# Gate products, last blocks and last mix of a two-layer encoder: three PSUM and queue edits

## The chip, the core and the metric

One NeuronCore of a Trainium2 chip runs the whole program in one launch. The metric is the device time of that launch in microseconds (us), lower is better. The core has five engines, each with its own in-order queue, that meet through semaphores: TensorE (PE in the profile, with its weight loads as PEld), VectorE (DVE), ScalarE (ACT), GpSimd (POOL) and SyncE (SP), which here only issues DMAs. Matmuls write to PSUM, which VectorE and ScalarE can read.

## The reference

One inference step of a two-layer encoder over 640 tokens (512 of a prompt, 8 x 16 of samples), model width 1024, all in float32:

```python
for l in range(2):
    h = rmsnorm(x, ln1);  u, va, qkv, z, b, a, ga, gb = split(h @ w_in)
    z_a = gelu(u) * spatial(layernorm(gelu(va)))        # branch A: chunked gMLP
    z_b = rmsnorm(gated_delta_rule(conv(qkv), ...)) * silu(z)   # branch B
    mix = sigmoid(ga) * (z_a @ p_a) + sigmoid(gb) * (z_b @ p_b)
    x = x + mix @ w_o
    x = x + square(relu(rmsnorm(x, ln2) @ w_up)) @ w_down
y = rmsnorm(x, final_norm)
```

This case is about the line `mix`, the product with `w_o` and the end of the product with `w_down`.

## The kernel before

Activations lie transposed: 1024 features as 8 chunks of 128 partitions, 640 tokens along the free axis, in two halves of 320 (`HT`). Every large product takes each operand as a high and a low part (`split`: ScalarE writes the high part, then VectorE writes the rest as the low part), and sums three matmuls: high x high, high weight x low activation, low weight x high activation. A block is 128 output features for all tokens: 2 halves x 8 chunks x 3 = 48 matmuls of 320 columns (`three`, called by `gemm`). A block's weights (512 KB) are loaded by SP into `raw` (three buffers) and split into `whi` and `wlo` (two buffers each), one block ahead of their use (`Feed`). So ScalarE can write a block's `whi` only when TensorE has finished the block two ahead of it.

PSUM has 8 banks: the tag `g` is a pair of two-bank tiles (`pair`, names `pg_...`), and the tags `c` and `d` are two one-bank tiles each (`bank`, names `ps_...`). A `gemm` fills a pair, one half of the tokens in each bank; two pairs take turns, so a block may start when the block two ahead of it has been read out of PSUM. All waits are kept per tile.

TensorE's order is the order of the program. The other engines' orders come from a scheduler with priorities: what stands in `tc.high_priority(offset=...)` is taken earlier by so many steps, the splits of weights among it.

The places of this change, in the order of the program, each once in a layer:

- `merge`, first loop (stage pb): `z_b @ p_b` in eight blocks. A gate tile `sg` (name `rg`) is loaded from the DRAM tensor `gd` by `gated`, and VectorE multiplies block `g` in PSUM by it into `mix[g]` (L1036). The gates of blocks 0 and 1 are loaded through GpSimd's queue. Ahead of this loop on VectorE runs the layer norm of branch A (L977 to L981, tile `vn`), whose powers GpSimd computes (L979).
- `merge`, second loop (stage pa): `z_a @ p_a`; VectorE multiplies by the other gate (L1046), GpSimd adds the product to `mix[m]` (L1047), and `split` writes chunk `m` of `Bh` and `Bl`.
- `residual_raw` (stage wo): `mix @ w_o`, whose every block needs all eight chunks of `Bh` and `Bl`. `take` adds a block to `x`, scales it (`hwo`), splits it into `Ah` and `Al` and adds its squares into the sum of the norm, the first seven blocks as a whole and the last one in two halves of 320 tokens. `rates` follows, within the first block of the stage up.
- `residual` (end of stage dn): the last 1024 rows of `w_down`, blocks 0 to 3 by `gemm`, and 4 to 7 by `group`: token half `a` = 0 first, then `a` = 1, each as two pair tiles (`i` = 0 and 1) that hold two blocks (`j` = 0 and 1) of that half. `add` adds a pair to `x`, squares it on ScalarE and sums the squares into `acca`, on GpSimd for half 0 and on VectorE for half 1. `finish` then computes the rate of a half (three small products `ps_msa`, a power on GpSimd, a spread `dga`, three products `ps_mra`) and scales that half: for layer 0 into the `Ah` and `Al` of the next layer's first stage (gf), for layer 1 into the output.

Of the kernel before, what the change touches and what calls it, by code (L numbers as in the profile page):

```python
# [11 lines left out]
AF = mybir.ActivationFunctionType  # L12
ALU = mybir.AluOpType
# [8 lines left out]
KC = 8  # L22
# [8 lines left out]
HT = NT // 2  # L31
# [8 lines left out]
AHEAD = 200  # L40
# [22 lines left out]
def encoder(ctx, tc, xin, wblk, wba, sct, sdelta, prow, pcol, gates, wst, bsr, convw, consts, delta0,  # L63
            y_out, conv_out, dp_out, ds_out, gv_out):
    nc = tc.nc
# [12 lines left out]
    def mm(out, lhsT, rhs, start, stop, pos=None):  # L78
        kw = {} if pos is None else {"tile_position": pos}
        nc.tensor.matmul(out, lhsT=lhsT, rhs=rhs, start=start, stop=stop, **kw)  # L80


    x = cp.tile([P, KC, NT], F32, name="x")
# [9 lines left out]
    half = (slice(0, HT), slice(HT, NT))  # L93
# [38 lines left out]
    def split(dst_hi, dst_lo, src):  # L132
        nc.scalar.activation(dst_hi, src, AF.Copy)  # L133
        nc.vector.tensor_tensor(dst_lo, src, dst_hi.bitcast(F32), op=ALU.subtract)  # L134
# [44 lines left out]
    def bank(tag, nm):  # L179
        return psp.tile([P, 512], F32, tag=tag, name=f"ps_{nm}")  # L180

    def pair(nm):
        return psp.tile([P, 2, 512], F32, tag="g", bufs=2, name=f"pg_{nm}")

    def three(ps, w, ah, al):

        hi, lo = (v[:].rearrange("p (k c) -> p k c", k=KC) for v in w)
        for a in range(2):
            n = slice(a * 320, (a + 1) * 320)
            for k in range(KC):  # L190
                mm(ps[:, a, :320], hi[:, k, :], ah[:, k, n], k == 0, False)
                mm(ps[:, a, :320], hi[:, k, :], al[:, k, n], False, False)
                mm(ps[:, a, :320], lo[:, k, :], ah[:, k, n], False, k == KC - 1)
                yield

    def gemm(l, b, ah, al, nm, use, halves=False):

        w = feed.take(l, b)
        ps = pair(nm)
        for u, _ in enumerate(three(ps, w, ah, al)):  # L200
            if halves and u % 8 == 7:
                use(ps, u // 8)
            elif u == 15:
                use(ps)
            yield

    def group(l, bs, ah, al, nm, use, pl, chunks=False):


        w = [feed.take(l, bs[0]), feed.take(l, bs[1], ahead=False)] + [feed.apart(l, b, pl) for b in bs[2:]]  # L210
        w = [[v[:].rearrange("p (k c) -> p k c", k=KC) for v in p] for p in w]
        order = [(j, k) for k in range(KC) for j in range(2)] if chunks else [(j, k) for j in range(2) for k in range(KC)]
        for a in range(2):
            for i in range(2):
                ps = pair(f"{nm}{a}{i}")
                for u, (j, k) in enumerate(order):
                    hi, lo = w[2 * i + j]
                    mm(ps[:, j, :HT], hi[:, k, :], ah[:, k, half[a]], k == 0, False)
                    mm(ps[:, j, :HT], hi[:, k, :], al[:, k, half[a]], False, False)
                    mm(ps[:, j, :HT], lo[:, k, :], ah[:, k, half[a]], False, k == KC - 1)  # L220
                    if (a, i, u) == (1, 1, 1):
                        feed.ahead()
                    if u % 2 and u < 15:
                        yield
                use(i, a, ps)
                yield

    def paced(work, n, ahead=AHEAD):
# [388 lines left out]
    halves = (slice(0, 64), slice(64, 128))  # L617
# [171 lines left out]
    v2 = lambda ap: ap.rearrange("p (a n) -> p a n", a=2)  # L789
# [160 lines left out]
    def merge(l, ond, msd, gd):  # L950
        with phase(f"merge{l}", 1) as pl:
            Bh = pl.tile([P, KC, NT], F32R, name=f"Bh{l}")
            Bl = pl.tile([P, KC, NT], F32R, name=f"Bl{l}")
            with phase(f"branch{l}", 1) as po:
# [9 lines left out]
                bs = rep_row(po, bsr[l], f"bs{l}", "bs")  # L964
# [42 lines left out]
                    run(zs)  # L1007

                with phase(f"sp{l}", 1) as pq:
                    def gated(i, m, eng=nc.sync):  # L1010
                        sg = pq.tile([P, NT], F32, tag="sg", bufs=3, name=f"rg{i}{l}{m}")
                        eng.dma_start(sg[:], gd[i, m])
                        return sg

                    def spatial(g):
                        u = gated(0, g)
                        b0, b1 = bank("dc"[g % 2], f"s{l}{g}a"), bank("dc"[g % 2], f"s{l}{g}b")
                        for t in range(5):
                            o = b0[:, t * P:(t + 1) * P] if t < 4 else b1[:, 0:P]
                            mm(o, vn[:, t, g * P:(g + 1) * P], ws[:, t // 4, g, :], True, True)  # L1020
                        s = pq.tile([P, NT], F32, tag="s", bufs=2, name=f"sp{l}{g}")
                        nc.vector.tensor_tensor(s[:, 0:512].rearrange("p (t n) -> p t n", t=4),
                                                b0[:].rearrange("p (t n) -> p t n", t=4), rep(bsv[:, g, :], 1, 4), op=ALU.add)
                        nc.vector.tensor_tensor(s[:, 512:640].rearrange("p (b n) -> p b n", b=8),
                                                b1[:, 0:P].rearrange("p (b n) -> p b n", b=8), rep(bsv[:, g, 0:16], 1, 8), op=ALU.add)
                        nc.gpsimd.tensor_tensor(s[:], s[:], u[:], op=ALU.mult)
                        split(Ah[:, g, :], Al[:, g, :], s[:])

                    with tc.high_priority(offset=2 * AHEAD):
                        ahead = [gated(1, g, nc.gpsimd) for g in range(2)]  # L1030
                    mix = [pq.tile([P, NT], F32, name=f"mix{l}{g}") for g in range(KC)]
                    for g in range(KC):
                        sg = ahead[g] if g < 2 else gated(1, g)

                        def pb(ps):
                            nc.vector.tensor_tensor(v2(mix[g][:]), ps[:, :, 0:HT], v2(sg[:]), op=ALU.mult)  # L1036

                        run(gemm(l, WB_PB + g, Bh, Bl, f"pb{l}{g}", pb))
                        for i in {3: (0, 1), 4: (2, 3), 5: (4, 5), 6: (6, 7)}.get(g, ()):
                            spatial(i)  # L1040
                    nc.sync.dma_start(gv_out[l], vn[:, 4, :])
                    for m in range(KC):
                        sg = gated(2, m)

                        def pa(ps):
                            nc.vector.tensor_tensor(v2(sg[:]), ps[:, :, 0:HT], v2(sg[:]), op=ALU.mult)  # L1046
                            nc.gpsimd.tensor_tensor(mix[m][:], mix[m][:], sg[:], op=ALU.add)  # L1047
                            split(Bh[:, m, :], Bl[:, m, :], mix[m][:])

                        run(gemm(l, WB_PA + m, Ah, Al, f"pa{l}{m}", pa))  # L1050
            es = ExitStack()
# [3 lines left out]
    def residual(l, b0, ah, al, nm, nrm):  # L1055

        def add(xs, ps, dst, first):
            nc.vector.tensor_tensor(xs, ps[:, :, 0:HT], xs, op=ALU.add)
            nrm.add(dst, xs, first, nc.vector if dst == 1 else nc.gpsimd)

        for m in range(4):
            run(gemm(l, b0 + m, ah, al, f"{nm}{m}", lambda ps: add(v2(x[:, m, :]), ps, None, m == 0)))
        with phase(f"g{nm}") as pw:
            g = group(l, range(b0 + 4, b0 + 8), ah, al, nm,
                      lambda i, a, ps: add(x[:, 4 + 2 * i:6 + 2 * i, half[a]], ps, a, False), pw)
            for _ in range(16):
                next(g)
            run(g, fin := nrm.finish(0))
            run(fin)
        return nrm.finish(1)  # L1070

    def residual_raw(l, b0, ah, al, nm, nrm):

        def take(m, n, ps, w, dst, eng):
            xs, h = w(x[:, m, n]), nrm.pl.tile([P, NT], F32, tag="h", bufs=2, name=f"h{nm}{m}")[:, n]
            nc.vector.tensor_tensor(xs, ps, xs, op=ALU.add)
            nrm.scaled(h, m, n)
            split(Ah[:, m, n], Al[:, m, n], h)
            nrm.add(dst, xs, m == 0, eng)

        for m in range(KC - 1):
            run(gemm(l, b0 + m, ah, al, f"{nm}{m}",
                     lambda ps: take(m, slice(0, NT), ps[:, :, 0:HT], v2, None, nc.gpsimd)))
        m = KC - 1
        run(gemm(l, b0 + m, ah, al, f"{nm}{m}",
                 lambda ps, a: take(m, half[a], ps[:, a, 0:HT], lambda v: v, a, nc.vector), halves=True))

        def rates():
            for n, a in ((1, 0), (2, 1)):
                for _ in range(n):  # L1090
                    yield
                yield from nrm.rate(a, 5)

        return rates()
# [148 lines left out]
```

## Time and profile before

| | us |
|---|---|
| Median of 3 runs (2514.13 to 2517.27) | 2514.52 |
| The profiled execution | 2513.98 |
| Span of its trace, first to last instruction | 2512.3 |
| TensorE busy, 98% of the span, 18456 matmuls | 2464.4 |
| VectorE, ScalarE and GpSimd busy | 1300.4, 1026.6 and 568.3 |
| Start of the stages pb, pa, wo and up in layer 0 | 612.39, 684.52, 740.84 and 800.47 |
| Start of the stages pb, pa, wo and up in layer 1 | 1852.58, 1924.19, 1980.51 and 2040.13 |
| Start of the stage gf of layer 1 | 1257.56 |

Busy time on TensorE is time in which a matmul is in flight; a matmul lasts about 0.31 us from its start to its end, and the next one starts 0.147 us after it where nothing waits. The idle time in brackets of a row is what the engine stood idle ahead of it, and after the arrow stands what ended that. `PEclk` is the TensorE clock that was granted, as a share of full speed. The start of a row is in us from the start of the span.

### The profile page before, as it was taken

Reading aid. Unit: us, or ns where it says so; the run is one execution under the profiler, and the core shown is the slowest. Engines: PE = TensorE matmul, PEld = TensorE weight load, DVE = VectorE, ACT = ScalarE, POOL = GpSimd, SP = SyncE. Lnnn points to the kernel's source line nnn. Section 1 sums busy time; section 2 is a strip of 40 time slices with the busy share of each in tenths; the row PEclk is TensorE's granted clock in tenths of the full one; section 3 lists DMA queues with packets and bytes.
Section 4 is the critical chain, followed back from the end, with each engine's and each line's share of the span. In section 5 each row is a group of like instructions: output and inputs, shape, how many; then the busy total and the mean of one; then the engine's idle time right before and its main releaser. Section 6 shows DMA issues by size and latency. Waiting matters only on the chain. (4 is left out here: it accounts for less than half of the span.)

```text
span 2512.3 us, 45051 instructions
## 1 busy us (share of the span) xinstructions
PE 2464.4 (98%) x18456; PEld 2387.2 (95%) x18456; DVE 1300.4 (52%) x2686; ACT 1026.6 (41%) x1968; POOL 568.3 (23%) x638
## 2 busy tenths in 40 slices
PE   8999999999999999999999999999999999999998
PEld 7999999998999999999999999999989999999997
DVE  6656776527455433333346677664275553333333
ACT  5767666533123212122347676774322222122122
POOL 0233433211222201011213343331112221011012
PEclk9999999999999999999999999999999999999999
DMA  5233333346532222222233333343564322222221
GB/s 175 83 107 122 103 96 99 115 132 228 167 95 74 72 75 74 76 76 76 85 94 115 102 96 96 101 127 113 164 204 145 92 68 76 76 76 76 73 71 67
DMA packets 124493, 261.28 MB, mean 104 GB/s; under 512 B 17232, under 2 KB 57072, under 8 KB 124288
## 3 DMA queue, kind: packets, MB, share of 16 engines
q1 hardware_dynamic: 123968, 257.10, 32.3%
q8 instruction: 145, 2.38, 0.4%
q0 software_dynamic: 320, 1.31, 0.2%
q14 instruction: 60, 0.49, 0.1%
HBM read 218.22 MB, written 40.15 MB: 103 GB/s over the span
## 5 line engine op out<-in xcount | busy, mean ns | idle before, releaser
L133 ACT ACTIVATE whi<-raw 128x1024 fp32r<-128x1024 f32 x304 | 321.8, 1059 | 1003.9 <-issue 369.6
L134 DVE TENSOR_TENSOR wlo<-raw,whi 128x1024 fp32r<-128x1024 f32 x304 | 397.8, 1309 | 167.8 <-ACT whi L133 153.6
L80 PE MATMUL pg_dn<-gl,whi 128*128 128x320 f32 x1024 | 316.6, 309 | 2.1 <-DVE gl L1111 2.1
L80 PE MATMUL pg_up<-Ah,whi 128*128 128x320 f32 x1024 | 317.1, 310 | 0.0
L80 PE MATMUL pg_dn<-gh,whi 128*128 128x320 f32 x1024 | 316.8, 309 | 0.0
L80 PE MATMUL pg_up<-Ah,wlo 128*128 128x320 f32 x1024 | 316.4, 309 | 0.0
L80 PE MATMUL pg_dn<-gh,wlo 128*128 128x320 f32 x1024 | 316.4, 309 | 0.0
L80 PE MATMUL pg_up<-Al,whi 128*128 128x320 f32 x1024 | 316.4, 309 | 0.0
L80 PE MATMUL pg_g<-Ah,whi 128*128 128x320 f32 x896 | 289.4, 323 | 1.3 <-ACT sg L821 1.3
L80 PE MATMUL pg_g<-Ah,wlo 128*128 128x320 f32 x896 | 276.9, 309 | 0.1
L80 PE MATMUL pg_g<-Al,whi 128*128 128x320 f32 x896 | 276.4, 308 | 0.0
L1110 POOL TENSOR_TENSOR r<-r 128x640 f32<-128x640 f32 x64 | 101.8, 1590 | 684.8 <-ACT gh L1109 684.8
L80 PE MATMUL pg_p<-Ah,whi 128*128 128x320 f32 x768 | 251.4, 327 | 0.0
L80 PE MATMUL pg_p<-Al,whi 128*128 128x320 f32 x768 | 237.0, 309 | 0.4 <-DVE Al L134 0.4
L80 PE MATMUL pg_p<-Ah,wlo 128*128 128x320 f32 x768 | 237.3, 309 | 0.0
L80 PEld LDWEIGHTS pg_dn<-gl,whi 128*128 128x128 f32 x1024 | 192.2, 188 | 2.6 <-DVE gl L1111 2.6
L80 PEld LDWEIGHTS pg_up<-Ah,whi 128*128 128x128 f32 x1024 | 192.2, 188 | 0.0
L80 PEld LDWEIGHTS pg_up<-Al,whi 128*128 128x128 f32 x1024 | 192.2, 188 | 0.0
L80 PEld LDWEIGHTS pg_dn<-gh,whi 128*128 128x128 f32 x1024 | 192.2, 188 | 0.0
L80 PEld LDWEIGHTS pg_dn<-gh,wlo 128*128 128x128 f32 x1024 | 192.2, 188 | 0.0
L80 PEld LDWEIGHTS pg_up<-Ah,wlo 128*128 128x128 f32 x1024 | 192.2, 188 | 0.0
L80 PEld LDWEIGHTS pg_g<-Ah,whi 128*128 128x128 f32 x896 | 168.6, 188 | 9.0 <-issue 3.5
(689 smaller groups left out, 5394.5 us busy)
## 6 DMA issues: line engine op xcount, KB each, us to landing
raw<-in_wblk SPq DMA_DIRECT2D x304, 512.0 KB, 3.6
gd<-sg SPq DMA_DIRECT2D x56, 320.0 KB, 3.5
rg<-gd SPq DMA_DIRECT2D x44, 320.0 KB, 3.3
S<-in_sdelta SPq DMA_DIRECT2D x16, 512.0 KB, 5.7
out<-S SPq DMA_DIRECT2D x16, 512.0 KB, 3.8
gr<-rowd SPq DMA_DIRECT2D x16, 320.0 KB, 5.0
er<-rowd SPq DMA_DIRECT2D x16, 320.0 KB, 4.0
ond<-osb SPq DMA_DIRECT2D x16, 320.0 KB, 2.2
```

Of the source, the lines that this page charges most:

```text
L80: nc.tensor.matmul(out, lhsT=lhsT, rhs=rhs, start=start, stop=stop, **kw)
L133: nc.scalar.activation(dst_hi, src, AF.Copy)
L134: nc.vector.tensor_tensor(dst_lo, src, dst_hi.bitcast(F32), op=ALU.subtract)
L1110: nc.gpsimd.tensor_tensor(r[:], r[:], r[:], op=ALU.mult)
```

## The change

Five edits, the first four in each layer.

1. The products of blocks 0 and 1 of stage pb are copied by ScalarE out of PSUM into `mix[g]`, and VectorE multiplies `mix[g]` by the gate in SBUF. Blocks 2 to 7 stay as they were.
2. The gates of blocks 0 and 1 are loaded by SP like the others, without priority; `mix` is allocated ahead of the gate tiles now.
3. The last block of stage pa: VectorE instead of GpSimd adds to `mix[7]`, in two halves of 320 tokens, and each half is split by itself.
4. The last block of stage wo goes into two one-bank tiles of tag `c`, one for each half of the tokens.
5. In `residual`, `i` = 1 of each half goes into two one-bank tiles of tag `c`, and each block is added, squared and summed as soon as it is complete (`single`). The squares of half 0 of `group` are now summed by VectorE too.

```diff
     def three(ps, w, ah, al):
...
+            out = ps[a][:, :320] if isinstance(ps, list) else ps[:, a, :320]
             for k in range(KC):
-                mm(ps[:, a, :320], hi[:, k, :], ah[:, k, n], k == 0, False)
...
+                mm(out, hi[:, k, :], ah[:, k, n], k == 0, False)
...
     def gemm(l, b, ah, al, nm, use, halves=False):
         w = feed.take(l, b)
-        ps = pair(nm)
+        ps = [bank("c", f"{nm}{a}") for a in range(2)] if halves else pair(nm)
         for u, _ in enumerate(three(ps, w, ah, al)):
             if halves and u % 8 == 7:
-                use(ps, u // 8)
+                use(ps[u // 8], u // 8)
...
-    def group(l, bs, ah, al, nm, use, pl, chunks=False):
+    def group(l, bs, ah, al, nm, use, pl, chunks=False, single=None):
...
-                ps = pair(f"{nm}{a}{i}")
+                apart = i == 1 and single is not None
+                if apart:
+                    ps = [bank("c", f"{nm}{a}{j}")[:, 0:HT] for j in range(2)]
+                else:
+                    both = pair(f"{nm}{a}{i}")
+                    ps = [both[:, j, 0:HT] for j in range(2)]
...
+                    if apart and k == KC - 1:
+                        single(j, a, ps[j])
...
-                use(i, a, ps)
+                if not apart:
+                    use(i, a, both)
...
-                    with tc.high_priority(offset=2 * AHEAD):
-                        ahead = [gated(1, g, nc.gpsimd) for g in range(2)]
                     mix = [pq.tile([P, NT], F32, name=f"mix{l}{g}") for g in range(KC)]
                     for g in range(KC):
-                        sg = ahead[g] if g < 2 else gated(1, g)
+                        sg = gated(1, g)
                         def pb(ps):
-                            nc.vector.tensor_tensor(v2(mix[g][:]), ps[:, :, 0:HT], v2(sg[:]), op=ALU.mult)
+                            if g < 2:
+                                nc.scalar.activation(v2(mix[g][:]), ps[:, :, 0:HT], AF.Copy)
+                                nc.vector.tensor_tensor(mix[g][:], mix[g][:], sg[:], op=ALU.mult)
+                            else:
+                                nc.vector.tensor_tensor(v2(mix[g][:]), ps[:, :, 0:HT], v2(sg[:]), op=ALU.mult)
...
                         def pa(ps):
                             nc.vector.tensor_tensor(v2(sg[:]), ps[:, :, 0:HT], v2(sg[:]), op=ALU.mult)
-                            nc.gpsimd.tensor_tensor(mix[m][:], mix[m][:], sg[:], op=ALU.add)
-                            split(Bh[:, m, :], Bl[:, m, :], mix[m][:])
+                            if m + 1 < KC:
+                                nc.gpsimd.tensor_tensor(mix[m][:], mix[m][:], sg[:], op=ALU.add)
+                                split(Bh[:, m, :], Bl[:, m, :], mix[m][:])
+                                return
+                            for n in half:
+                                nc.vector.tensor_tensor(mix[m][:, n], mix[m][:, n], sg[:, n], op=ALU.add)
+                                split(Bh[:, m, n], Bl[:, m, n], mix[m][:, n])
...
         def add(xs, ps, dst, first):
-            nc.vector.tensor_tensor(xs, ps[:, :, 0:HT], xs, op=ALU.add)
-            nrm.add(dst, xs, first, nc.vector if dst == 1 else nc.gpsimd)
+            nc.vector.tensor_tensor(xs, ps if len(ps.shape) == 2 else ps[:, :, 0:HT], xs, op=ALU.add)
+            nrm.add(dst, xs, first, nc.gpsimd if dst is None else nc.vector)
...
-                      lambda i, a, ps: add(x[:, 4 + 2 * i:6 + 2 * i, half[a]], ps, a, False), pw)
+                      lambda i, a, ps: add(x[:, 4 + 2 * i:6 + 2 * i, half[a]], ps, a, False), pw,
+                      single=lambda j, a, ps: add(x[:, 6 + j, half[a]], ps, a, False))
...
-                 lambda ps, a: take(m, half[a], ps[:, a, 0:HT], lambda v: v, a, nc.vector), halves=True))
+                 lambda ps, a: take(m, half[a], ps[:, 0:HT], lambda v: v, a, nc.vector), halves=True))
```

Where the instructions stand. First ScalarE at the start of stage pb of layer 0, before: `whi` from `raw_42` to `raw_45` are the high parts of the weights of blocks 2 to 5, `vn` is the GELU of the stage before.

```order
L972 ACTIVATE vn_6970<-pg_va01a 128x512 x2
L133 ACTIVATE whi<-raw_42_7351 128x1024
L133 ACTIVATE whi<-raw_43_7448 128x1024
L133 ACTIVATE whi<-raw_44_7504 128x1024
L133 ACTIVATE whi<-raw_45_7562 128x1024
```

and now:

```order
L983 ACTIVATE vn_6970<-pg_va01a 128x512 x2
L133 ACTIVATE whi<-raw_42_7351 128x1024
L133 ACTIVATE whi<-raw_43_7446 128x1024
L1046 ACTIVATE mix_7432<-pg_pb_7448 128x640
L1046 ACTIVATE mix_7433<-pg_pb_7507 128x640
L133 ACTIVATE whi<-raw_44_7505 128x1024
```

The two copies of edit 1 stand behind the weight part of block 3 (`raw_43`) and ahead of that of block 4. The two multiplications on VectorE stand where the old ones stood.

Second VectorE at the end of stage pa of layer 0 (`rg` is the gated product of the last block, `wlo` from `raw_81` the low part of the weights of wo's block 1, `hwo` and `x` the first block of wo), before:

```order
L1046 TENSOR_TENSOR rg_8452<-pg_pa_8460,rg_8452 128x640
L134 TENSOR_TENSOR wlo<-raw_81_8397,whi 128x1024
L134 TENSOR_TENSOR Bl_6966<-mix_7443,Bh_6965 128x640
L1076 TENSOR_TENSOR x<-pg_wo_8526,x 128x640
L332 TENSOR_SCALAR hwo_8575<-x,col 128x640
```

and now:

```order
L1059 TENSOR_TENSOR rg_8454<-pg_pa_8462,rg_8454 128x640
L1065 TENSOR_TENSOR mix_7439<-mix_7439,rg_8454 128x320
L134 TENSOR_TENSOR wlo<-raw_81_8399,whi 128x1024
L134 TENSOR_TENSOR Bl_6966<-mix_7439,Bh_6965 128x320
L1065 TENSOR_TENSOR mix_7439<-mix_7439,rg_8454 128x320
L134 TENSOR_TENSOR Bl_6966<-mix_7439,Bh_6965 128x320
L1095 TENSOR_TENSOR x<-pg_wo_8531,x 128x640
```

The first half's addition has come ahead of the split of the weights, and its low part right behind that split.

Third VectorE at the end of the program (`ha` is the scaled output of half 0, the last `sta` opens the rate of half 1), before:

```order
L303 TENSOR_TENSOR acca_25018<-acca_25018,sqa_25451 128x320
L352 TENSOR_TENSOR ha_25420<-ha_25420,ps_mra_25455 128x640
L1058 TENSOR_TENSOR x<-pg_dn_25461,x 128x2x320
L303 TENSOR_TENSOR acca_25018<-acca_25018,sqa_25519 128x320 x2
L314 TENSOR_SCALAR sta_25541<-ps_msa_25537 128x3
```

and now:

```order
L314 TENSOR_TENSOR acca_25038<-acca_25038,sqa_25475 128x320
L363 TENSOR_TENSOR ha_25444<-ha_25444,ps_mra_25479 128x640
L1076 TENSOR_TENSOR x<-ps_dn_25485,x 128x320
L314 TENSOR_TENSOR acca_25038<-acca_25038,sqa_25520 128x320
L1076 TENSOR_TENSOR x<-ps_dn_25486,x 128x320
L314 TENSOR_TENSOR acca_25038<-acca_25038,sqa_25548 128x320
L325 TENSOR_SCALAR sta_25569<-ps_msa_25565 128x3
```

Behind the last matmul now come one addition and one sum of half the size, where one addition of a pair and two sums came. On SP the loads of the first three gates (`rg`) have come ahead of the load of block 6's weights and of the output of `vn`; TensorE's order is unchanged.

More of the change, by code (lines that the diff above doesn't have):

```diff
@@ L189, in three @@
             n = slice(a * 320, (a + 1) * 320)
+            out = ps[a][:, :320] if isinstance(ps, list) else ps[:, a, :320]
             for k in range(KC):
-                mm(ps[:, a, :320], hi[:, k, :], ah[:, k, n], k == 0, False)
-                mm(ps[:, a, :320], hi[:, k, :], al[:, k, n], False, False)
-                mm(ps[:, a, :320], lo[:, k, :], ah[:, k, n], False, k == KC - 1)
+                mm(out, hi[:, k, :], ah[:, k, n], k == 0, False)
+                mm(out, hi[:, k, :], al[:, k, n], False, False)
+                mm(out, lo[:, k, :], ah[:, k, n], False, k == KC - 1)
                 yield
@@ L214, in group @@
             for i in range(2):
-                ps = pair(f"{nm}{a}{i}")
+                apart = i == 1 and single is not None
[4 more added lines that the diff above has]
+                    ps = [both[:, j, 0:HT] for j in range(2)]
                 for u, (j, k) in enumerate(order):
                     hi, lo = w[2 * i + j]
-                    mm(ps[:, j, :HT], hi[:, k, :], ah[:, k, half[a]], k == 0, False)
-                    mm(ps[:, j, :HT], hi[:, k, :], al[:, k, half[a]], False, False)
-                    mm(ps[:, j, :HT], lo[:, k, :], ah[:, k, half[a]], False, k == KC - 1)
+                    mm(ps[j], hi[:, k, :], ah[:, k, half[a]], k == 0, False)
+                    mm(ps[j], hi[:, k, :], al[:, k, half[a]], False, False)
+                    mm(ps[j], lo[:, k, :], ah[:, k, half[a]], False, k == KC - 1)
                     if (a, i, u) == (1, 1, 1):
                         feed.ahead()
+                    if apart and k == KC - 1:
+                        single(j, a, ps[j])
                     if u % 2 and u < 15:
                         yield
-                use(i, a, ps)
+                if not apart:
+                    use(i, a, both)
                 yield
@@ L1009, in merge, with gated @@
                 with phase(f"sp{l}", 1) as pq:
-                    def gated(i, m, eng=nc.sync):
+                    def gated(i, m):
                         sg = pq.tile([P, NT], F32, tag="sg", bufs=3, name=f"rg{i}{l}{m}")
-                        eng.dma_start(sg[:], gd[i, m])
+                        nc.sync.dma_start(sg[:], gd[i, m])
                         return sg
```

## The prediction

> **What bounds the kernel.** I read the page's busy times first, then the waits of TensorE alone, then the timeline of the engines around each of those waits.
>
> ```profile
> PE 2464.4 (98%) x18456; PEld 2387.2 (95%) x18456; DVE 1300.4 (52%) x2686; ACT 1026.6 (41%) x1968; POOL 568.3 (23%) x638
> ```
>
> TensorE carries the time: no other engine passes 52%. The change takes no matmul away, so it can win only where TensorE stands still or runs slowly. Its waits (us in total, times, longest), three rows that the change touches:
>
> ```profile
> PE pg_pb L80 <- DVE mix L1036: 9.7, 2, 4.9
> PE ps_msa L80 <- DVE acca L303: 4.5, 2, 2.9
> PE pg_wo L80 <- DVE x L1076: 3.2, 2, 1.6
> ```
>
> Each comes once per layer. A wait also costs what follows it; busy times, granted clock (PEclk) and DMA in stretches of pa, of pb in both layers, of wo's last half block, and of the second layer's start (gf):
>
> ```profile
> 684.60:740.80 56.20, 56.20 (x385) 56.20 (x384) 31.23 (x23) 13.68 (x15) 11.03 (x7) 1.00 0.37 111
> 626.40:631.50 5.10, 0.23 (x3) 0.04 (x1) 3.65 (x4) 1.06 (x1) 2.06 (x3) 0.72 0.56 155
> 631.50:635.50 4.00, 4.00 (x15) 4.00 (x16) 0.82 (x1) 0.00 (x0) 0.00 (x0) 0.50 1.02 399
> 1871.70:1874.60 2.90, 2.90 (x11) 2.90 (x12) 0.82 (x1) 0.00 (x0) 0.00 (x0) 0.51 1.01 380
> 796.80:800.40 3.60, 3.55 (x24) 3.56 (x25) 1.28 (x3) 0.83 (x2) 0.00 (x0) 1.00 0.08 31
> 1263.60:1267.00 3.40, 1.90 (x14) 1.90 (x15) 1.57 (x4) 0.60 (x2) 0.79 (x1) 0.99 0.78 249
> 1267.00:1270.40 3.40, 3.40 (x16) 3.40 (x15) 0.56 (x1) 0.39 (x1) 0.06 (x1) 0.50 0.15 59
> ```
>
> Undisturbed, as in pa, a matmul starts every 56.20 / 385 = 0.146 us, a block of 48 in 7.04 us. After the idle 5 us of pb the clock is at half, and TensorE does 15 matmuls in 4.00 us (27 at full speed) and 11 in 2.90 (20): 12 x 0.146 = 1.75 us and 9 x 0.146 = 1.3 us more. After the 1.6 us wait in wo it stays at 1.00, and the 24 matmuls of that half block take 3.60 instead of 3.50: 0.1 us is what a restart costs.
>
> **Edits 1 and 2, the copy by ScalarE (stage pb).** The timeline of layer 0:
>
> ```profile
> 612.63 1.06 ACT L133 ACTIVATE whi<-raw 128x1024 fp32r<-128x1024 f32 x1 [2.17 <-PE pg_va01a L80]
> 613.60 1.07 ACT L972 ACTIVATE vn<-pg_va01a 128x512 f32<-128x512 f32 x2
> 626.31 0.31 PE L80 MATMUL pg_pb<-Bh,wlo 128*128 128x320 f32 x1
> 626.51 1.06 ACT L133 ACTIVATE whi<-raw 128x1024 fp32r<-128x1024 f32 x1 [5.93 <-PE pg_pb L80]
> 627.15 1.31 POOL L1012 DMA_DIRECT2D rg<-gd  x2
> 628.44 1.22 DVE L134 TENSOR_TENSOR wlo<-raw,whi 128x1024 fp32r<-128x1024 f32 x1
> 629.69 0.89 SPq L146 DMA_DIRECT2D raw<-in_wblk  x1
> 630.52 0.82 DVE L1036 TENSOR_TENSOR mix<-pg_pb,rg 128x640 f32<-128x640 f32 x1 [0.86 <-DMA rg<-gd]
> 631.49 0.61 PE L80 MATMUL pg_pb<-Bh,whi 128*128 128x320 f32 x1 [4.87 <-DVE mix L1036]
> ```
>
> Block 2 wants the pair of block 0, which was complete long before. VectorE multiplies it only at 630.52, behind the layer norm and a weight split, and then behind the gate's load, which GpSimd issued at 627.15, after its last power for that norm. Block 2 starts 631.49 - 626.31 = 5.18 us after the matmul ahead of it, 5.03 more than 0.146.
>
> Now ScalarE empties the pair. In its order the copy stands behind block 3's `whi`, which waits for the end of block 1 (626.51). The next instruction on ScalarE starts 613.60 - 612.63 = 0.97 us after a `whi`: copy at 627.48. Its price has a row of the same form, a Copy of a pair to SBUF:
>
> ```profile
> L862 ACT ACTIVATE sf<-pg_gf x2: 704/704/705, 18.4 to 32.3; 128x640 f32<-128x640 f32 x2
> ```
>
> So it ends at 628.18 and block 2 starts at about 628.24: a gap of 1.93, still 1.8 us lost. The edit removes two thirds of the wait, not all of it. I price the clock's fall at nothing for 1.8 us idle (the rival below takes the other end) and add 0.1 for the restart. Saved in layer 0: 5.03 + 1.75 - 1.9 = 4.9; in layer 1, whose wait is as long, 5.03 + 1.3 - 1.9 = 4.4. Together 9.3.
>
> What else moves: the two multiplications, now from SBUF, stay in their place on VectorE (0.82 each from L1036 serves as their price), and nothing but block 2's own product stands behind them; their gates, now issued by SP, no longer wait for GpSimd's powers. Block 6's `raw`, issued at 629.69, now stands behind three gate loads on SP, but it also waits for the `wlo` that ends at 629.66, and its use is four blocks (28 us) off. ScalarE's next `whi` waits for block 2's end anyway. All hidden.
>
> **Edit 3, the last mix in halves (end of pa).**
>
> ```profile
> 741.04 0.82 DVE L1046 TENSOR_TENSOR rg<-pg_pa,rg 128x640 f32<-128x640 f32 x1 [2.75 <-PE pg_pa L80]
> 741.94 1.57 POOL L1047 TENSOR_TENSOR mix<-mix,rg 128x640 f32<-128x640 f32 x1 [5.47 <-DVE rg L1046]
> 741.98 2.61 DVE L134 TENSOR_TENSOR wlo<-raw,whi 128x1024 fp32r<-128x1024 f32 x1
> 743.55 0.74 ACT L133 ACTIVATE Bh<-mix 128x640 fp32r<-128x640 f32 x1 [1.60 <-POOL mix L1047]
> 744.34 0.41 PE L80 MATMUL pg_wo<-Bh,whi 128*128 128x320 f32 x1 [0.26 <-ACT Bh L133]
> 745.39 0.42 PE L80 MATMUL pg_wo<-Bl,whi 128*128 128x320 f32 x1 [0.64 <-DVE Bl L134]
> ```
>
> An idle time plus the 0.31 of the matmul ahead, less 0.146, is the loss: 0.26 + 0.64 + 2 x 0.16, and 0.1 for the restart: 1.3 us per layer. Note the `wlo` of 2.61 us beside GpSimd's 1.57; alone it took 1.22 at 628.44. With the half prices of the next fence (0.49 for a sum or low part, 0.46 for a high part): half addition 741.9 to 742.4, `wlo` to 743.5, high part on ScalarE to 742.9, low part 743.45 to 743.95. TensorE wants them at about 743.92 and 744.07, and the second half of the tokens 3.5 us later. So the wait goes, by a margin of 0.1: saved 2 x 1.3 = 2.6, at worst 1.
>
> **Edit 4, the last block of wo in two banks.**
>
> ```profile
> 794.91 0.31 PE L80 MATMUL pg_wo<-Bh,wlo 128*128 128x320 f32 x1
> 796.31 0.48 DVE L1076 TENSOR_TENSOR x<-pg_wo,x 128x320 f32<-128x320 f32 x1
> 796.85 0.42 PE L80 MATMUL pg_wo<-Bh,whi 128*128 128x320 f32 x1 [1.62 <-DVE x L1076]
> 797.26 0.46 ACT L133 ACTIVATE Ah<-hwo 128x320 fp32r<-128x320 f32 x1
> 797.46 0.49 DVE L303 TENSOR_TENSOR accb<-accb,sqb 128x320 f32<-128x320 f32 x1 [0.25 <-ACT sqb L292]
> ```
>
> The second half of the block goes into the other bank of the same tile, and waits until VectorE has read the first. In two tiles nothing of this block reads what it writes. Saved: 796.85 - 794.91 - 0.146 + 0.1 = 1.9 per layer, 3.8 together. Late next is the rate in the first block of up; it depends on the end of wo's last block and moves with it. The `c` tiles were last used in stage pb, over 90 us earlier.
>
> **Edit 5, the group at the end of dn.** The end of the program:
>
> ```profile
> 2494.74 2.83 ACT L343 ACTIVATE ha<-x,col 128x320 f32<-128x320 f32 x6 [3.33 <-DMA out<-ha]
> 2497.42 0.82 DVE L1058 TENSOR_TENSOR x<-pg_dn,x 128x640 f32<-128x640 f32 x1 [2.77 <-PE pg_dn L80]
> 2498.34 0.74 ACT L295 ACTIVATE sqa<-x 128x640 f32<-128x640 f32 x1 [0.77 <-DVE x L1058]
> 2499.11 1.02 DVE L303 TENSOR_TENSOR acca<-acca,sqa 128x320 f32<-128x320 f32 x2 [0.86 <-ACT sqa L295]
> 2500.28 0.80 PE L80 MATMUL ps_msa<-cst,acca 128*128 128x1 f32 x6 [2.89 <-DVE acca L303]
> ```
>
> Everything from 2497.42 on is a chain. It shrinks by 0.82 - 0.48, 0.74 - 0.47 (the half square takes a half `Ah`'s time) and 1.02 - 0.49: 1.1 us at most. But in ScalarE's new order seven of the `ha` scalings and the first square stand ahead of the last square on ScalarE, from 2494.74 on at 2.83 / 6 = 0.47 or less each: free at 2498.3 instead of 2498.0. I take 0.8 us. In layer 0 TensorE waits 1.56 us for the two sums, in the same way:
>
> ```profile
> 1261.76 2.36 DVE L134 TENSOR_TENSOR wlo<-raw,whi 128x1024 fp32r<-128x1024 f32 x2 [0.30 <-ACT whi L133]
> 1264.04 1.01 DVE L303 TENSOR_TENSOR acca<-acca,sqa 128x320 f32<-128x320 f32 x2
> 1265.10 0.83 PE L80 MATMUL ps_msa<-cst,acca 128*128 128x1 f32 x6 [1.56 <-DVE acca L303]
> ```
>
> One of the sums now goes ahead of the two weight splits, so the last ends 0.5 earlier: saved 0.5 (0 to 1). The sums of half 0, moved from GpSimd to VectorE, meet an engine with idle time there.
>
> **Sum.** 9.3 + 2.6 + 3.8 + 0.8 + 0.5 = 17.0 us from the profiled execution's 2513.98: 2497.0. That execution lies 0.54 under the median; the runs spread over 3.1 us, so I leave it at 2497.0.
>
> **Rivals.** (a) The clock falls after the remaining 1.8 us too. For it speaks gf: after a wait of 1.56 us and a few one-column matmuls the clock went to 0.50 for 3.4 us (the stretch 1267.00). Against it, the wait of 1.62 us in wo was followed by 1.00 (the stretch 796.80). A stretch of 3.4 us at half speed costs 1.7, in both layers 3.4: 2500.4. Chance 0.18. [...]
>
> (b) The reverse: edit 5 shortens gf's wait so far that its half clock goes as well. 16 matmuls in 3.40 instead of 23 are 7 x 0.146 = 1.0 us, and the chain's whole 1.1 comes: 2495.6. Chance 0.12.
>
> (c) One of the edits 3 and 4 doesn't do what it says (the halves come too late, or the second bank still waits): 2.6 or 3.8 back, 2499.6 to 2500.8. Chance 0.10.
>
> (d) No change: block 2 still waits for its multiplication, as if the copy didn't free the pair. Then the three others save 17.0 - 9.3 = 7.7; under 5 us would need edit 4 to fail too. Chance 0.04.
>
> (e) Slower. In edit 5 VectorE's `x` of the last block stands behind a sum that waits for a square, and this square on ScalarE behind a scaling that waits for an output DMA (2494.74). If that DMA landed after 2497.9, every us more would be added to the end. To end slower it would have to land 17 us later than it did; its wait is 3.33. Chance 0.03.
>
> The forecast keeps 0.53. About 0.2%, or 5 us, is what a measurement can tell from no change here. Range: 2494.0 to 2503.0, from (b) with 1.6 us for a shorter wait in pb and the spread of runs, to (a) with the worst case of edit 3 (1.6) and 1 us of spread. Faster 0.93, same 0.04, slower 0.03.
>
> **What would show it.** Right: the wait of `pg_pb` on VectorE's `mix` is replaced by one on ScalarE's `mix` of 1.6 us per layer, with PEclk near 1.00 behind it; no `pg_wo` waits are left; `ps_msa` at the end starts 2.1 us after VectorE's last addition to `x` does, instead of 2500.28 - 2497.42 = 2.9. Wrong: a wait of 4 us or more left in pb, or a new row among TensorE's waits for a `ps_wo` or `ps_dn` tile.

## The result, and the profile after

The changed kernel takes 2493.53 us (median of 4 runs, 2492.47 to 2494.07), the kernel before beside it 2514.32 (2512.91 to 2517.27): a ratio of 0.9915, 95% interval 0.9898 to 0.9932. That is 20.8 us faster; 17.0 were forecast, and the range ended 0.5 us above the time. The profiled execution took 2493.33, its span is 2491.5. One run of edit 3 alone (2992.75 us) and one of the kernel before (4856.16 us) lie far above all others of their kernels and count in no median of this document.

The page's busy times, then TensorE's waits (total, times, longest):

```profile
PE 2456.1 (99%) x18456; PEld 2380.7 (96%) x18456; DVE 1302.2 (52%) x2704; ACT 1029.9 (41%) x1978; POOL 557.8 (22%) x624
```

```profile
PE pg_pb L80 <- ACT mix L1046: 3.2, 2, 1.6
PE ps_msa L80 <- DVE acca L314: 3.0, 2, 2.0
...
PE ps_va L80 <- ACT whi L133: 0.8, 1, 0.8
```

The 9.7 us for VectorE's `mix` have become 3.2 for ScalarE's, all rows for `pg_wo` are gone, the two waits for the sums are down from 4.5 to 3.0, and a wait for a weight split is new in a stage that the change doesn't touch. Stage by stage, each from the first matmul of a stage to that of the next in the two timelines (us, and what was forecast for the difference; heads and va are the stages between gf and pb, which no edit touches):

| stage | before | after | difference | forecast |
|---|---|---|---|---|
| first stage of layer 0 (gf) | 42.76 | 41.14 | -1.62 | 0 |
| heads of layer 0 | 507.91 | 506.98 | -0.93 | 0 |
| va of layer 0 | 55.28 | 56.54 | +1.26 | 0 |
| pb, both layers | 143.74 | 134.15 | -9.59 | -9.3 |
| wo, both layers | 119.25 | 112.68 | -6.57 | -6.4 |
| first stage of layer 1 (gf) | 34.29 | 32.18 | -2.11 | -0.5 |
| heads and va of layer 1 | 560.73 | 560.31 | -0.42 | 0 |
| last dn blocks to the end | 74.00 | 73.27 | -0.73 | -0.8 |
| pa, up and the rest of dn | 967.85 | 967.82 | -0.03 | 0 |

The place in pb where block 2 waited, now (timeline of layer 0; the matmul rows are the last of block 1 and the first of block 2):

```profile
625.06 0.31 PE L80 MATMUL pg_pb<-Bh,wlo 128*128 128x320 f32 x1
625.26 1.06 ACT L133 ACTIVATE whi<-raw 128x1024 fp32r<-128x1024 f32 x1 [5.93 <-PE pg_pb L80]
626.22 1.28 ACT L1046 ACTIVATE mix<-pg_pb 128x640 f32<-128x640 f32 x2
626.96 0.42 PE L80 MATMUL pg_pb<-Bh,whi 128*128 128x320 f32 x1 [1.59 <-ACT mix L1046]
627.18 1.22 DVE L134 TENSOR_TENSOR wlo<-raw,whi 128x1024 fp32r<-128x1024 f32 x1
628.32 1.55 DVE L1047 TENSOR_TENSOR mix<-mix,rg 128x640 f32<-128x640 f32 x2
```

The copy starts 0.96 us after the `whi` ahead of it and takes 0.692 (median of its four rows); block 2 starts 1.90 us after block 1's last matmul, where 1.93 was forecast. VectorE's two multiplications start 1.4 us after block 2 does, and nobody waits for them. Busy times and clock (PEclk) behind that wait, and in wo's last half block:

```profile
626.96:630.46 3.50, 3.50 (x24) 3.50 (x25) 2.91 (x4) 0.54 (x1) 0.00 (x0) 1.00 0.66 222
788.60:792.20 3.60, 3.60 (x28) 3.60 (x26) 2.84 (x8) 2.11 (x4) 0.00 (x0) 1.00 0.21 83
```

The clock is 1.00 in both, as forecast. The start of wo, and the end of the program:

```profile
735.58 0.49 DVE L1065 TENSOR_TENSOR mix<-mix,rg 128x320 f32<-128x320 f32 x1
735.99 1.22 DVE L134 TENSOR_TENSOR wlo<-raw,whi 128x1024 fp32r<-128x1024 f32 x1
736.11 0.47 ACT L133 ACTIVATE Bh<-mix 128x320 fp32r<-128x320 f32 x1 [0.47 <-DVE mix L1065]
737.13 0.48 DVE L134 TENSOR_TENSOR Bl<-mix,Bh 128x320 fp32r<-128x320 f32 x1
...
2477.44 0.49 DVE L1076 TENSOR_TENSOR x<-ps_dn,x 128x320 f32<-128x320 f32 x1 [1.26 <-PE ps_dn L80]
2478.28 0.46 ACT L303 ACTIVATE sqa<-x 128x320 f32<-128x320 f32 x1
2478.76 0.49 DVE L314 TENSOR_TENSOR acca<-acca,sqa 128x320 f32<-128x320 f32 x1 [0.83 <-ACT sqa L303]
2479.40 0.80 PE L80 MATMUL ps_msa<-cst,acca 128*128 128x1 f32 x6 [2.00 <-DVE acca L314]
```

The low part is there at 737.61, and TensorE, which reached wo at 734.52, wants it 22 matmuls later, at 737.74: the wait is gone by 0.13 us (0.1 forecast). At the end the sums go to TensorE 1.96 us after the last addition to `x` starts, instead of 2.86 (2.1 forecast). The signs of a wrong forecast, a wait of 4 us left in pb or one for a `ps_wo` or `ps_dn` tile, stand nowhere among the waits.

### The profile page after: what moved, and what is told of

Same layout as the page of the kernel before. It is cut to its first block, busy times and chain, and to the rows that moved or that the text cites. A ratio compares the mean times of both kernels' runs of the same rounds, so it can differ in the third digit from the quotient of the medians.

```text
span 2491.5 us, 45066 instructions
## 1 busy us (share of the span) xinstructions
PE 2456.1 (99%) x18456; PEld 2380.7 (96%) x18456; DVE 1302.2 (52%) x2704; ACT 1029.9 (41%) x1978; POOL 557.8 (22%) x624
## 5 line engine op out<-in xcount | busy, mean ns | idle before, releaser
L80 PE MATMUL pg_dn<-gl,whi 128*128 128x320 f32 x960 | 296.8, 309 | 2.1 <-DVE gl L1130 2.1
L80 PE MATMUL pg_dn<-gh,whi 128*128 128x320 f32 x960 | 296.8, 309 | 0.0
L80 PE MATMUL pg_dn<-gh,wlo 128*128 128x320 f32 x960 | 296.6, 309 | 0.0
L80 PEld LDWEIGHTS pg_dn<-gl,whi 128*128 128x128 f32 x960 | 180.2, 188 | 2.6 <-DVE gl L1130 2.6
L80 PEld LDWEIGHTS pg_dn<-gh,whi 128*128 128x128 f32 x960 | 180.3, 188 | 0.0
L80 PEld LDWEIGHTS pg_dn<-gh,wlo 128*128 128x128 f32 x960 | 180.2, 188 | 0.0
```

## The experiments

What was open: the two gf rows, the heads and va of layer 0 missed. In both gf stages the clock differs between the two profiles: at half for 6.83 us before (21.09 to 27.92) and for 3.41 now (22.79 to 26.21) in layer 0, for 3.41 before (1266.95 to 1270.37) and not at all now in layer 1. va has the new wait of 0.8 us for a weight split, and the heads hold none of the edits. **Main theory at first**: the edits' stages add up, and the excess at the start of layer 1 came from the shorter wait there, which no longer lets the clock fall. **Rival**: whether the clock falls there is set by when the wait falls in time. Out of the first four runs came a third form of it, the **theory of the window**, an estimate from the clock records. Between its start and its end, the profile of before has half clock from 21.09 to 27.92, 628.66 to 635.49, 1266.95 to 1270.37 and 1871.11 to 1874.53 us, and all these edges lie whole multiples of 3.413 us apart. The theory cuts a run into windows at such edges and expects half clock for one window when TensorE did too little in the window before.

**Each edit alone, on the kernel before.** Edits 1 and 2:

```diff
-                        ahead = [gated(1, g, nc.gpsimd) for g in range(2)]
...
+                            if g < 2:
+                                nc.scalar.activation(v2(mix[g][:]), ps[:, :, 0:HT], AF.Copy)
+                                nc.vector.tensor_tensor(mix[g][:], mix[g][:], sg[:], op=ALU.mult)
```

> The kernel before with edits 1 and 2 alone (the copies of the first two gate products by ScalarE, all gates issued by SP). Main theory (the stages add up, and each edit is worth what its own stage lost): 9.5 us faster; the pb stages take 67.1 us each instead of 72.1 and 71.6, TensorE waits there once per layer for ScalarE's mix, 1.6 us, and the clock stays near 1.00 behind it; the waits for wo's x (3.2 us in all) and the 1.56 us wait of ps_msa with a half clock behind it stay. Rival (the half clock at the second layer's start is set by when things fall in time, and not by the wait): the shift by 5 us of all that follows can take the half clock away there too, 11.0 us faster.

Measured: 2502.23 us (4 runs) against 2513.21 (25 runs of before in that batch); ratio 0.9958 (0.9943 to 0.9973), 11.0 us. The pb stages take 67.08 and 67.07. The stage at the start of layer 1 stays at 34.29 with its half clock, so the rival's case did not come in this run; yet 11.0 is 1.4 more than the 9.6 that the stages of the first two profiles give. The next three runs tell why: they keep pb as it was.

Edit 3 alone:

```diff
+                            for n in half:
+                                nc.vector.tensor_tensor(mix[m][:, n], mix[m][:, n], sg[:, n], op=ALU.add)
+                                split(Bh[:, m, n], Bl[:, m, n], mix[m][:, n])
```

> The kernel before with edit 3 alone (the last mix by VectorE in halves). Main theory: 2.6 us faster, 1.3 per layer; no wait of pg_wo for Bh or Bl at the start of wo; the wait of pb (4.9 us) and the half clock behind it stay. Rival (the halves only move the wait to the second half of the tokens): 0 to 1 us faster, with a new wait in wo's first block.

Edit 4 alone:

```diff
-        ps = pair(nm)
+        ps = [bank("c", f"{nm}{a}") for a in range(2)] if halves else pair(nm)
```

> The kernel before with edit 4 alone (wo's last block in two single-bank tiles). Main theory: 3.8 us faster, 1.9 per layer, the wait of pg_wo for x gone. Rival (the wait hid something that is late next, the rate in the first block of up): 1 to 2 us faster, with a new wait at the start of up.

Edit 5 alone:

```diff
+                if apart:
+                    ps = [bank("c", f"{nm}{a}{j}")[:, 0:HT] for j in range(2)]
...
+            nrm.add(dst, xs, first, nc.gpsimd if dst is None else nc.vector)
```

> The kernel before with edit 5 alone (the group's last block in single tiles, the sums of half 0 on VectorE). Main theory (the shorter wait of ps_msa at the second layer's start, 1.0 instead of 1.56 us, keeps the clock up): 2.9 us faster, 0.8 at the program's end and 2.1 at the layer boundary, with PEclk near 1.00 behind the wait. Rival (the half clock there depends on where the wait falls in time, and edit 5 shortens the wait only): 1.3 us faster, the wait 1.0 us and the half clock of 3.4 us still behind it.

Measured: 2510.07 us for edit 3 (ratio 0.9986, 0.9976 to 0.9995), 2510.41 for edit 4 (0.9986, 0.9977 to 0.9995), 2511.48 for edit 5 (0.9994, 0.9985 to 1.0004, so not told from no change by the times). These are 3.1, 2.8 and 1.7 us under the median of before, each good to some 2.4 us; the stages tell more. TensorE's waits of 700 to 880 us, of edit 3 alone and then of edit 4 alone:

```profile
PE pg_wo L80 <- DVE x L1081: 1.6, 1, 1.6
PE ps_mrb L80 <- DVE dgb L317: 1.0, 1, 1.0
```

```profile
PE ps_mrb L80 <- DVE dgb L318: 1.0, 1, 1.0
PE pg_wo L80 <- DVE Bl L134: 0.6, 1, 0.6
PE pg_wo L80 <- ACT Bh L133: 0.3, 1, 0.3
```

Each takes away its own wait and no more. wo falls from 59.6 to 58.25 and 58.23 us with edit 3 (2.8 in both layers, 2.6 forecast) and to 57.75 twice with edit 4 (3.75; 3.8 forecast). Two things differ from the expectations. In pb, which none of the three touches, layer 1 took 72.96, 73.73 and 72.92 us and not 71.61: the wait lasts 5.1 to 5.9 from matmul to matmul, and the half clock behind it 2.9 to 6.0 us. And the stage at the start of layer 1 took 32.71 and 32.73 with edits 3 and 4, without the half clock, although the wait is as long as before. With edit 5 it took 32.17. So edit 5's own share is 32.72 - 32.17 = 0.55 us, as forecast, and the half clock's is 34.29 - 32.72 = 1.57, and comes or stays away without any edit there.

**Edit 1 without edit 2** (copies by ScalarE, the two gates still issued by GpSimd):

```diff
                         sg = ahead[g] if g < 2 else gated(1, g)
...
+                                nc.scalar.activation(v2(mix[g][:]), ps[:, :, 0:HT], AF.Copy)
```

> The kernel before with edit 1 alone: the copies by ScalarE, the first two gates still issued by GpSimd ahead of time. Main theory (the copy frees the pair, where the gates are issued doesn't matter to TensorE): as edits 1 and 2 together, 2502.2 within 2 us, the pb stages 67.1 us. Rival (without edit 2 GpSimd's late gate still holds VectorE, and VectorE the weight split of block 3): pb stages over 68 us, with a wait for wlo or mix in block 3 or 4.

Measured: 2503.02 us (ratio 0.996, 0.9945 to 0.9975), pb 67.08 in both layers. The first multiplication waits for its gate until 632.46 (1.29 us on the DMA), and TensorE doesn't notice. So edit 1 makes the gain; edit 2 is worth nothing that shows.

**Edit 5 taken back from the changed kernel**, profiled three times, and the changed kernel again:

```diff
-            nrm.add(dst, xs, first, nc.gpsimd if dst is None else nc.vector)
+            nrm.add(dst, xs, first, nc.vector if dst == 1 else nc.gpsimd)
...
-                      single=lambda j, a, ps: add(x[:, 6 + j, half[a]], ps, a, False))
```

> The changed kernel without edit 5 (edits 1 to 4). Theory of the window: TensorE waits 1.56 us for the sums at the second layer's start and then has 0.7 us of one-column products, 2.4 us without full work, of which over 2.0 us fall into one window in half of the phases. So the stage from the first gf matmul to the first of the heads takes 34.3 us in about half of the runs and 32.7 us in the others, told by the grid of the same run, and 32.2 with edit 5 in all runs: the time is 0.8 (end of program) + 0.5 + 0 or 1.6 over the changed kernel, 2494.9 or 2496.5. Rival (edit 5 is worth the 1.3 us that were forecast, in every run): 2494.8 with a spread like that of the changed kernel, the stage always the same.

> The same kernel a second time, for another phase of the window. Theory of the window: 34.3 or 32.7 us for the stage at the second layer's start, by the grid read off the half clocks of the first stage. Rival: the same as in the first run.

> The same kernel a third time. Theory of the window: as for the second; of the three runs together with the five seen so far without edit 5 (two with the half clock there, three without), about half show it. Rival: the same in all three.

> The changed kernel once more, on the same chip as the one without edit 5. Theory of the window: the stage at the second layer's start 32.2 us again and no half clock there or in pb, whatever the phase; the first stage, which the change doesn't touch, anywhere between 41.0 and 43.0 us, as its half clock lasts longer or shorter by the phase. Rival (the first stage's 1.6 us came from the change): 41.1 us again.

Measured: without edit 5 2496.79 us (5 runs; the two single runs took 2501.18 and 2497.08), with it 2493.8 (5 runs): 3.0 apart (0.73 at the end, 0.55 and half of 1.57 would be 2.1). The stage at the start of layer 1 takes 34.28, 34.30 and 32.73 us in the three profiles of one and the same kernel, and 32.17 in the changed one. The wait, in the first and in the third of them:

```profile
1255.18 0.83 PE L80 MATMUL ps_msa<-cst,acca 128*128 128x1 f32 x6 [1.57 <-DVE acca L304]
```

```profile
1257.52 0.83 PE L80 MATMUL ps_msa<-cst,acca 128*128 128x1 f32 x6 [1.56 <-DVE acca L304]
```

The same wait; but busy time and clock in stretches of 3.413 us, cut at the edges on which the clock changes in the record of the same run (first profile: its first stage runs at half clock in 23.69:27.10):

```profile
23.69:27.10 3.41, 3.41 (x15) 3.41 (x14) 2.55 (x7) 0.74 (x1) 0.00 (x0) 0.50 0.40 149
1252.49:1255.90 3.41, 1.84 (x15) 1.58 (x13) 2.60 (x4) 1.79 (x4) 0.00 (x0) 1.00 0.42 147
1255.90:1259.31 3.41, 3.41 (x14) 3.41 (x15) 0.72 (x2) 0.00 (x0) 0.85 (x1) 0.50 0.42 161
1259.31:1262.73 3.42, 3.42 (x27) 3.42 (x26) 1.31 (x2) 1.05 (x2) 1.27 (x1) 1.00 0.21 79
```

and the third:

```profile
1253.36:1256.77 3.41, 2.60 (x17) 2.33 (x17) 3.12 (x4) 3.27 (x5) 0.00 (x0) 1.00 0.05 12
1256.77:1260.18 3.41, 2.66 (x19) 2.67 (x20) 1.38 (x4) 0.00 (x0) 0.85 (x1) 1.00 0.76 291
1260.18:1263.60 3.42, 3.42 (x27) 3.42 (x26) 1.39 (x2) 1.05 (x2) 1.35 (x1) 1.00 0.25 93
```

In the first profile one window holds nearly all of the pause (1.84 us busy, and of its 15 products some have one column), and the next one runs at 0.50 from edge to edge; in the third the pause is shared by two windows (2.60 and 2.66 busy) and nothing follows. With edit 5 the wait is 1.04 us. In the profile of edit 5 alone the whole pause falls into one window too, and the clock stays:

```profile
1265.41 0.80 PE L80 MATMUL ps_msa<-cst,acca 128*128 128x1 f32 x6 [1.04 <-DVE acca L312]
1263.78:1267.19 3.41, 2.37 (x19) 2.14 (x18) 1.64 (x3) 1.35 (x3) 0.70 (x1) 1.00 0.74 187
1267.19:1270.60 3.41, 3.41 (x27) 3.41 (x26) 1.08 (x2) 1.05 (x2) 0.63 (x2) 1.00 0.29 120
```

Over all runs without edit 5 the half clock was there in 4 of 8 profiles, with it in none of 6. The rival that expected the same in every run is out, and so is any rule by the length of the wait alone: 1.57 us had the half clock behind it in the first profile, 1.56 had none in the third. In the changed kernel the first stage, 41.14 in its first profile, takes 42.93 in this one: its 1.62 us in the table above were luck. In the seven profiles in which it takes 41.0 to 41.5 us its last half clock lasts one window, in the seven with 42.8 to 43.1 two.

**A longer wait in pb** (the changed kernel with two, then four, more copies of block 0's product ahead of the real one, into tiles that are overwritten later):

```diff
+                                for i in range(2 if g == 0 else 0):
+                                    nc.scalar.activation(v2(mix[7 - i][:]), ps[:, :, 0:HT], AF.Copy)
```

> The changed kernel with two more copies of block 0's product (into tiles that are overwritten later) ahead of the real one on ScalarE, so that the wait in pb grows from 1.6 to about 2.9 us, an idle time of some 3.05. Theory of the window (the clock is set anew every 3.41 us, on a grid that runs free of the program and has another phase in each run; a window in which TensorE did under 41% of the work it can do at full clock is followed by one at half clock): whether the half clock follows depends on the phase, in 72% of phases; the grid read off the half clocks of the first stage of the same run must tell which, in each layer by itself. [...] With half clock behind the wait a stage is up to 1.6 us longer.

> The changed kernel with four more copies ahead of the real one, so that the wait in pb grows to about 4.2 us, an idle time of some 4.35. Theory of the window: over 2.0 us of it lie in one window at any phase, so half clock follows in both layers, and pb stages take 70.5 to 72 us. [...]

Measured: 2498.11 and 2500.66 us, one run each. With two copies TensorE waits 2.8 us in each layer, and the half clock follows in both. Windows between the clock's edges in that run: one pair in the first stage, then pb in layer 0 and in layer 1:

```profile
19.14:22.55 3.41, 1.23 (x6) 0.97 (x7) 3.02 (x6) 2.97 (x6) 0.00 (x0) 1.00 0.40 136
22.55:25.97 3.42, 3.42 (x15) 3.42 (x14) 3.08 (x8) 1.19 (x2) 0.00 (x0) 0.50 0.50 156
623.30:626.71 3.41, 0.75 (x6) 0.48 (x4) 2.98 (x3) 2.77 (x5) 1.32 (x1) 1.00 0.56 190
626.71:630.13 3.42, 3.31 (x12) 3.31 (x13) 1.84 (x3) 0.65 (x2) 0.00 (x0) 0.50 0.72 218
1855.51:1858.92 3.41, 0.63 (x6) 0.37 (x4) 2.98 (x3) 2.92 (x5) 1.18 (x1) 1.00 0.51 167
1858.92:1862.34 3.42, 3.42 (x13) 3.42 (x14) 1.69 (x3) 0.51 (x1) 0.00 (x0) 0.50 0.78 237
```

The stages take 69.75 and 69.80: 2.7 more than 67.07, 1.2 for the longer wait and 1.5 for the clock. With four copies the wait is 4.0 us, the half clock lasts one window in layer 0 and two in layer 1 (it ends at 631.13 and 1866.75, 362.0 windows apart), and the stages take 70.99 and 71.98: equal waits, 1 us apart.

**A faster version**: the changed kernel with block 2 of pb in two single-bank tiles, so that it waits for no copy.

```diff
+                        def apart(ps, a):
+                            nc.vector.tensor_tensor(mix[g][:, half[a]], ps[:, 0:HT], sg[:, half[a]], op=ALU.mult)
-                        run(gemm(l, WB_PB + g, Bh, Bl, f"pb{l}{g}", pb))
+                        run(gemm(l, WB_PB + g, Bh, Bl, f"pb{l}{g}", apart if g == 2 else pb, halves=g == 2))
```

> The changed kernel with block 2 of pb in two single-bank tiles as well, so that it waits for no copy; block 3, 7 us later, is the first to need the pair that ScalarE empties. Main theory (the 1.6 us wait of pb that is left is pure loss): no wait of pg_pb or ps_pb, the pb stages 65.2 us each instead of 67.1, 3.7 us faster than the changed kernel, 2490. Rival (the wait covers something else, such as the weights of block 3 or the spatial products that need the same banks): 0 to 2 us faster, with a new wait in block 3 or at the first spatial product.

Measured: 2490.25 us (4 runs, 2489.1 to 2490.91), ratio to the kernel before 0.9907 (0.9892 to 0.9922). No run of the changed kernel stands beside it; that one's medians are 2493.53 and 2493.8. No wait for a `pb` tile is left; the stages take 65.23 and 65.22, 3.7 us less than in the changed kernel. ScalarE empties block 0's pair as late as before, but block 3 is the first to want it, 5 us after.

## Why the prediction missed by a little

The mechanisms were those of the prediction, and four of its five terms came out: pb 9.6 (9.3 forecast, with the copy at the place and the price it was given), edit 3 2.8 (2.6), edit 4 3.75 (3.8), the end 0.73 (0.8). Together edits 3 and 4 gave 6.57. Rival (a), the clock falling behind the 1.6 us that are left in pb, came in none of the 14 stages that have this wait (two in each of seven profiles, all 67.07 or 67.08 us); rivals (c), (d) and (e) did not come.

The step that failed is the layer boundary in edit 5: 0.5 forecast, 2.11 in the two profiles. Its first half, a sum half a microsecond earlier, is right (0.55 from edit 5 alone). The other half is rival (b), which had 0.12: the half clock behind that wait goes. Its price was too low as well: it took 1.0 us from a row of 16 matmuls (1267.00:1270.40), four of which are products of 128 columns, where rival (a) took 1.7 for the same time at half speed; measured were 1.57. Above all, the prediction priced the clock by the length of a wait, with gf's 1.56 us (half clock) set against wo's 1.62 (none), and left the contradiction open. The theory of the window resolves it by an estimate, with the limit of about 2.0 us of a window without full work that is worked out in the last section from the counts of 14 profiles. In gf the wait is followed by some 0.7 us of one-column products, so 2.4 us pass without full work; over 2.0 us of them fall into one window in (3.41 + 2.42 - 2 x 2.01) / 3.41 = 53% of phases, if every phase is equally likely; 4 of 8 profiles had it. wo's and pb's 1.6 us with the matmul's own start make under 1.8, which stays under that limit in any window. Edit 5 brings gf to about 1.9, just under: the emptiest window there had 0.43 of full work. By this estimate the half clock was in the profile of before by chance, edit 5 saves it in about half of the runs, and its fair price was 0.55 + 0.53 x 1.57 = 1.4, not 0.5.

The rest of the miss is the range's lower end. It lay 1.6 us under rival (b), for a shorter wait in pb and the spread of runs together, but stages that the change doesn't touch differ by more: over 14 profiles the first stage of layer 0 takes 41.0 to 43.1 us (how long its half clocks last), the heads of layer 0 506.0 to 508.0 and va of layer 0 55.3 to 58.4 (the longest with a half clock of its own). In this pair they made -1.62, -0.93 and +1.26, with the second layer's -0.42 together -1.7. Lastly the 9.3 us of edits 1 and 2 came out by luck. The prediction took the half clock behind the wait in pb from one profile, and that one was short in pb: its 143.7 us were 145.3, 146.1 and 144.9 in the three other profiles that keep pb, so with it the mean is 145.0 and the mean gain 145.0 - 134.15 = 10.8, which is what edits 1 and 2 alone showed in the times (11.0). Over all runs the kernel before has a median of 2513.44 (45 runs) and the changed one 2493.74 (9 runs): 19.7, of which the prediction, made from one profile, saw 17.0: short by 1.5 in pb, by 0.9 at the layer boundary, and by 0.2 in wo.

## What to carry to other kernels

Before a stall's price is taken from one profile, look at the same stage in several: here one wait of 1.56 us had either none or one window of half clock behind it, and waits of 5.1 to 5.9 us had 2.9 to 6.0 us. In this kernel the clock's share went with a shorter wait: none of the six profiles with edit 5 (a wait of about 1.0 us) shows it at the layer boundary, and none of the 14 stages with 1.6 us in pb, where 2.8 us had it in both layers. Taking the last 1.6 us away too gave 1.85 us a stage (67.07 to 65.22), about the wait itself. And where an engine frees a tile too late, another tile for the next block took the whole wait away (3.7 us more), where a faster reader had left a third of it.

## What the runs showed of the hardware

In each run all changes of the granted clock lie whole multiples of 3.413 us apart, to 0.001 us, over its whole length. The place of the edges differs from run to run: taken modulo 3.413 us from the first instruction they lie at 0.61 in the profile of before and at 2.31 in that of the changed kernel. Without edit 5 (first profile) the half clock of the first stage ends at 27.10 us and that of layer 1 at 1259.31, 361.0 windows apart; with the two extra copies the half clocks end at 25.97, 630.13 and 1862.34, the last two 177.0 and 538.0 windows after the first.

A window's work is counted here as 0.1465 us for each 320 columns, as a share of 3.413 us; at half clock the count spreads a matmul's work over twice the time, where the starts lie 0.267 us apart (the profile of before, 1267.10 to 1269.50). In the 14 profiles all 62 windows with under 0.39 of full work (from the first matmul on, with matmuls in the window behind) were followed by one at half clock, 8 of the 17 with 0.39 to 0.43, and none of the 295 with 0.43 to 0.72. From these counts comes the estimate used above: a limit between 1.95 and 2.08 us of a window without full work, (1 - 0.43) x 3.413 and (1 - 0.39) x 3.413. The emptiest windows at the layer boundary with edit 5 had 0.431, at the upper end of that band. That a one-column product counts by its column is part of the count and was not tested apart. By the waits alone: 2.8 us in pb brought the half clock in both layers of the run with two extra copies, and 1.56 us with one-column products behind it in 4 of 8 profiles.

Not settled is why the weights of untouched stages land later in some runs: in the changed kernel's first profile one `whi` in va of layer 0 starts 33.9 us after the first matmul of that stage, in the profile of before 31.8, and in both it had waited for its `raw`.
